# Five pairs of gate tiles from seven block products, ahead of the attention heads, in a transformer block in one kernel

## The chip, the cores and the metric

The kernel runs on one core of a Trainium2 chip. Its time is the device time of one execution in microseconds (us); the time before is the median of three runs. TensorE (PE) does the matrix products and its own weight loads (PEld), VectorE (DVE) and ScalarE (ACT) the elementwise work, GpSimd (POOL) a little of it, and SyncE (SP) issues nearly all DMA transfers, in order, on one queue.

## The reference

One transformer block over 1024 tokens of 1024 channels, 16 heads of 64, cut to what matters here:

```python
h = rms_norm(x, norm1_g)
glu_in, q, k, v, gate_logits = split(h @ w_in)        # 2048, 1024, 1024, 1024, 2048 columns
a = silu(rms_norm(causal_depthwise_conv(a_val * sigmoid(a_gate)), conv_norm_g))   # width 31
y_a = a @ w_conv_out
# q, k normed per head; three dilated windows (128/1, 512/4, 2048/16) with ALiBi,
# joined by their log-sum-exp: one softmax with a mask over all keys
o = attention(q, k, v)
y_b = o @ w_attn_out
g_a, g_b = split(sigmoid(gate_logits + gate_b))        # 1024 and 1024 columns
x = x + (g_a * y_a + g_b * y_b) @ w_out
x = x + feed_forward(rms_norm(x, norm2_g))             # 1024 -> 2 x 2816 -> 1024
```

All products are wanted in float32 accuracy. The kernel splits each factor into a rounded high part and the rest, and adds three products: high by high, high by low, low by high.

## The kernel before

**The gate product.** The logits of the gate are 16 tiles of 128 channels by 1024 tokens. For one tile and one half of the tokens `gemm_half` runs eight *steps*, one for each 128 input channels, of three matmuls with 512 columns (L111, L112, L113), 24 matmuls in all. The 16 tiles with their two halves are 768 matmuls. The conv output product `co` has eight such tiles, 384 matmuls. The generator `side_steps` lists both kinds in order, first the gates and then the conv output, 384 steps in all; each `next` issues one step. When a gate half is done, ACT copies it with the bias `C_GB` added (L210) and SP stores it to `dgate`; a tile's weights (`raw_gt`) are loaded ahead and split in four pieces, ACT rounding (`hi_gt`) and DVE subtracting (`lo_gt`), by `piece_high` and `piece_low`.

**Where the steps go.** After the q, k and v products, `cover` issues 43 of the steps (`COVER`) ahead of the heads, between the two small products of the conv branch's norm (`pss`, `psr`). 280 or so go into the heads: `FILL` gives for each of a head's eight slots how many steps are added, 17.5 a head, 60% of them before the slot's transposes and 40% after its output products. The rest, 37, run behind the last head, beside the first loads of the output projection.

**The heads.** A head has two halves of 512 queries, each half four slots of 128. In a slot, for queries i, `score` issues the products s (L697, L698), DVE adds the mask and takes the row minimum (L702), ACT does the exponential (L707), DVE the reciprocal (L710), and POOL scales the row (`share`, L711). Five slots later (`BACK`) the scaled rows are transposed on TensorE (`flip`, tile pp, L717), and ACT and DVE split the transposed block into `ph` (L79) and `pl` (L80). One slot on, `weigh` multiplies them by v (tile o, L731 and L732). The product has v's high and low part side by side as its 128 columns, so o holds two blocks of 64 rows which are added: `result` copies one with ACT to `ot` (L742), adds it on DVE (L743) and, for two heads together, stores the half to `do`. ACT's, DVE's and TensorE's instructions are issued in the order in which the code of this stage is written (`manual_schedule`); elsewhere a scheduler orders each engine.

**Around them.** A head's q, k and mask tiles are loaded by SP one head ahead, v half a head ahead. Before the heads, DVE does the width-31 convolution (L556) beside the q, k and v products. Behind the heads, `load_split` loads `do` half by half, splits it into `oT` and `merge` multiplies by the attention output weights; for that the gates are loaded and go through ACT's sigmoid.

The feed-forward's up-projection already works by pairs of tiles and seven block products; there `product` issues one block product of 12 matmuls (4 blocks of 128, three matmuls each).

Of the kernel before, what the change touches and what calls it, by code (L numbers as in the profile page):

```python
# [21 lines left out]
P = 128  # L22
D = 1024
# [12 lines left out]
FILL = (1.5, 3.4, 1.8, 1.9, 1.6, 3.0, 2.1, 2.2)  # L36
BACK = 5
SHARE = 0.6
COVER = (15, 8, 20)
# [14 lines left out]
def block_kernel(ctx: ExitStack, tc: tile.TileContext, x, xT, x0, g2, pack, mask,  # L54
# [76 lines left out]

    def spill(dst, src):
        sp.dma_start(dst.bitcast(F32), src.bitcast(F32))
# [7 lines left out]
    dv = [dr.tile([P, 8, 8, P], F32R, name=f"dv{i}") for i in range(2)]  # L141
    dgate = [dr.tile([P, T], F32, name=f"dgate{i}") for i in range(16)]
    da = dr.tile([P, KT, T], F32, name="da")
    dya = [dr.tile([P, T], F32, name=f"dya{i}") for i in range(8)]
    do_ = dr.tile([P, KT, T], F32, name="do")
# [33 lines left out]
    def side_steps(hT, da):  # L179
# [18 lines left out]
        def gate(c, half):  # L198
            def go(w):
                gp = bank_ps(f"gate_{c}_{half}")  # L200
                if c >= 12 and half == 1:
                    if not aT:
                        aT.extend(hb_tiles(hb1, "aT"))
                    ask_conv(0, 2 * (c - 12))
# [5 lines left out]
                act.activation(sg, gp, AF.Identity, bias=pk[:, C_GB + c : C_GB + c + 1])  # L210
# [19 lines left out]
        for c in range(12):  # L230
            for half in range(2):
                gate(c, half)
        for half in range(2):
            for c in range(12, 16):
                gate(c, half)
        for c0 in (0, 4):
            for half in range(2):
                for c in range(c0, c0 + 4):
                    conv_out(c, half)
# [5 lines left out]
        for i, (_, n, go) in enumerate(uses):  # L245
# [7 lines left out]
            if n.startswith("co"):  # L253
                need = max(need, marks[(i - 32) // 4 % 2])
# [25 lines left out]
    with tc.tile_pool(name="ph1", bufs=1) as p1:  # L280
# [157 lines left out]
        with tc.manual_schedule(engines={ENG.Activation, ENG.DVE, ENG.PE}):  # L438
# [30 lines left out]
            for k in range(KT):  # L469
# [5 lines left out]
                low(1, k)  # L475
                if k == 6:
                    factors(0)
# [13 lines left out]
            for k in range(KT):  # L491
# [3 lines left out]
                settled1 = low(0, k)  # L495
        pair(1, 1, range(8), HH + HL + LH, 1)
# [124 lines left out]
        p2i_cm = tc.tile_pool(name="ph2i", bufs=1, side="right", reuse_waits="tile")  # L621
        p2i = p2i_cm.__enter__()

        def head(h):
            hp, r, g8 = h // 2, (h % 2) * DH, h // 8
            q = p2i.tile([P, T], F32R, tag="q", bufs=2, name=f"q_{h}")
            kh = p2i.tile([P, T], F32R, tag="kh", bufs=2, name=f"kh_{h}")
            kl = p2i.tile([P, T], F32R, tag="kl", bufs=2, name=f"kl_{h}")
            m = p2i.tile([P, T], F32, tag="m", bufs=2, name=f"m_{h}")
# [7 lines left out]
        tiles = {0: head(0)}  # L637
        gates = side_steps(hT, da)

        def cover(n):  # L640
            for _ in range(n):
                next(gates)
                one_piece()

        cover(COVER[0])
# [12 lines left out]
        dgs = p1.tile([P, CW - 1 + T], F32, tag="apad", bufs=10, name="dgs")[:, 0:T].rearrange("p (a b) -> p a b", a=8)  # L658
        dve.tensor_tensor(out=dgs, in0=ident.unsqueeze(1).to_broadcast([P, 8, P]),
                          in1=rs8.unsqueeze(2).to_broadcast([P, 8, P]), op=ALU.mult)  # L660
        for tt in range(8):
            if tt % 4 == 0:
                psr = bank_ps(f"psr_{tt}")
            spread2 = pe.matmul(psr[:, (tt % 4) * P : (tt % 4 + 1) * P], ones, dgs[:, tt, :], start=True, stop=True)
            if tt % 4 == 3:
                dve.tensor_copy(sqacc[:, (tt // 4) * 512 : (tt // 4) * 512 + 512], psr)
        for c in range(8):
            ct = conv_acc[c]
            dve.tensor_tensor(out=ct, in0=ct, in1=sqacc, op=ALU.mult)
            ordered = conv_acc[c - 2] if c > 1 else p1.tile([P, CW - 1 + T], F32, tag="apad", bufs=10, name=f"ca_{c}")[:, 0:T]  # L670
            act.activation(turns(ordered), ct.rearrange("p (s m) -> p s m", s=2), AF.Silu,
                           scale=pk[:, C_CG + c : C_CG + c + 1])
            act.dma_start(da[:, c, :], ordered)
        cover(COVER[2])


    with tc.tile_pool(name="ph2", bufs=1, reuse_waits="tile") as p2:
# [3 lines left out]
        def ready2(tag, shape, dt, bufs, name):  # L681
            return laid.pop(tag) if tag in laid else p2.tile(shape, dt, tag=tag, bufs=bufs, name=name)

        def values(h):
            vals[h] = p2.tile([P, 8, P], F32R, tag="v", bufs=2, name=f"v_{h}")
# [38 lines left out]
        outs, opairs, read_out = {}, {}, {}  # L724
# [706 lines left out]
```

## Time and profile before

| | |
|---|---|
| time, three runs | 1744.08, 1743.93, 1745.34 us; median 1744.08 |
| span of the profiled execution (first to last instruction) | 1741.8 us, 2.3 us under the median of the runs |
| TensorE matmul busy | 1737.4 us (100%) |
| DVE, ACT, POOL busy | 1301.5 (75%), 797.1 (46%), 174.5 us (10%) |
| first gate step | 457.3 us |
| heads, first to last group of eight transposes for keys 0 of half 1 | 511.96 to 884.91 us |
| attention output product | from 928.5 us |

The profile is of one execution. A row of the timeline gives start, length, engine, line, operation, tile written and tiles read; matmuls are pipelined, so a row's length is longer than the distance to the next start, which is what counts. A row of a group has after its count the sum in us and the mean in ns.

### The profile page before, as it was taken

The numbers are of one execution on the slowest core, as the hardware profiler recorded it, in microseconds if no ns is written. First come the engines' busy times: TensorE is split into PE (matmuls) and PEld (weight loads), VectorE is DVE, ScalarE is ACT, GpSimd is POOL, SyncE is SP. The second block draws the span as 40 slices with busy tenths as digits, with TensorE's granted clock in tenths as the row PEclk, the third lists the DMA queues.
The fourth block names the chain that finished last, engine by engine and source line by source line (L and its number), as shares of the span: only waits on it lengthen the run. The fifth ranks groups of instructions, "written<-read, shape, count | busy, mean of one in ns | idle before, by whom it ended". The sixth has DMA issues, their size and how long they took to land.

```text
span 1741.8 us, 22805 instructions
## 1 busy us (share of the span) xinstructions
PE 1737.4 (100%) x8207; PEld 1449.2 (83%) x8207; DVE 1301.5 (75%) x2005; ACT 797.1 (46%) x1276; POOL 174.5 (10%) x188
## 2 busy tenths in 40 slices
PE   9999999999999999999999999999999999999999
PEld 7888888888888888888888888888888888888887
DVE  5999999999756666677654573787777776889873
ACT  5421233323276666667663342555445544633431
POOL 0000232132012222222200000000000000000000
PEclk9999999999999999999999999999999999999999
DMA  7211145345686456657456576632222222398851
GB/s 295 73 54 50 53 135 170 109 140 175 174 274 180 148 159 168 179 161 225 128 179 210 178 271 236 218 121 73 97 80 77 85 85 85 127 362 310 295 176 49
DMA packets 149633, 276.99 MB, mean 159 GB/s; under 512 B 12048, under 2 KB 61840, under 8 KB 149520
## 3 DMA queue, kind: packets, MB, share of 16 engines
q1 hardware_dynamic: 147072, 269.11, 47.1%
q10 hardware_dynamic: 2448, 6.42, 0.9%
q8 instruction: 64, 1.05, 0.2%
q14 instruction: 49, 0.40, 0.1%
HBM read 202.09 MB, written 73.40 MB: 158 GB/s over the span
## 4 chain that ended last, share of the span: by engine, by line
PE 99%; DMA 0%; SPq 0%; DVE 0%; issue 0%; ACT 0%; DVEq 0%; ACTq 0%
PE dx L1243 7%; PE xz L976 6%; PE xz L975 6%; PE xz L977 6%; PE dy L1243 5%; PE qkv L130 5%; PE qkv L128 5%; PE qkv L129 5%; PE pp L717 4%; PE gate L111 3%; PE gate L112 3%; PE gate L113 3%; PE y L976 2%; PE y L977 2%; PE y L975 2%; PE o L732 2%
## 5 line engine op out<-in xcount | busy, mean ns | idle before, releaser
L80 DVE TENSOR_TENSOR pl<-pp,ph 128x512 fp32r<-128x512 f32 (+2 forms) x191 | 100.2, 553 | 90.1 <-ACT ph L79 90.0
L128 PE MATMUL qkv<-hi_qkv,hT 128*128 128x512 f32 x384 | 151.0, 394 | 0.0
L130 PE MATMUL qkv<-hi_qkv,hT 128*128 128x512 f32 x384 | 150.2, 392 | 0.0
L129 PE MATMUL qkv<-lo_qkv,hT 128*128 128x512 f32 x384 | 149.6, 391 | 0.0
L79 ACT ACTIVATE ph<-pp 128x512 fp32r<-128x512 f32 (+2 forms) x191 | 86.7, 489 | 115.9 <-PE pp L717 115.6
L702 DVE CUSTOM_DVE_ANT_0 p<-s,m 128x128 f32<-128x128 f32 (+3 forms) x120 | 90.5, 754 | 44.1 <-PE s L698 39.7
L711 POOL TENSOR_SCALAR p<-p,st 128x128 f32<-128x128 f32 (+3 forms) x120 | 90.3, 752 | 281.7 <-DVE st L710 222.4
L1146 DVE SCALAR_TENSOR_TENSOR u<-u,pk 128x1023 f32<-128x1023 f32 x88 | 112.3, 1278 | 1.2 <-ACT u L1144 0.9
L111 PE MATMUL gate<-hT,hi_gt 128*128 128x512 f32 x256 | 102.3, 400 | 0.0
L112 PE MATMUL gate<-hT,hi_gt 128*128 128x512 f32 x256 | 100.4, 392 | 0.0
L113 PE MATMUL gate<-hT,lo_gt 128*128 128x512 f32 x256 | 100.3, 393 | 0.0
L104 POOL TENSOR_TENSOR rs<-ss,mhalf 128x8 f32<-128x8 f32 x32 | 67.0, 2096 | 295.7 <-DVE ss L103 295.6
L707 ACT ACTIVATE p<-p,st 128x128 f32<-128x128 f32 (+3 forms) x120 | 93.0, 775 | 2.7 <-DVE st L702 2.0
L556 DVE SCALAR_TENSOR_TENSOR cacc<-csum,both,cacc 128x512 f32<-128x512 f32 x120 | 89.5, 746 | 1.2 <-ACT cacc L554 0.9
L556 DVE SCALAR_TENSOR_TENSOR cacc<-apad,pk,cacc 128x512 f32<-128x512 f32 x120 | 87.6, 745 | 0.0
L130 PEld LDWEIGHTS qkv<-hi_qkv,hT 128*128 128x128 f32 x384 | 72.1, 188 | 14.9
L129 PEld LDWEIGHTS qkv<-lo_qkv,hT 128*128 128x128 f32 x384 | 72.2, 188 | 14.4
L80 DVE TENSOR_TENSOR lo_uv<-raw_uv,hi_uv 128x1024 fp32r<-128x1024 f32 x20 | 24.5, 1226 | 79.7 <-ACT hi_uv L79 79.7
L128 PEld LDWEIGHTS qkv<-hi_qkv,hT 128*128 128x128 f32 x384 | 72.1, 188 | 14.1
L556 DVE SCALAR_TENSOR_TENSOR codd<-apad,pk,codd 128x513 f32<-128x513 f32 x112 | 83.7, 748 | 0.0
L717 PE MATMUL pp<-ident,p 128*128 128x128 f32 x540 | 78.9, 273 | 0.0
L717 PEld LDWEIGHTS pp<-ident,p 128*128 128x128 f32 x540 | 65.6, 140 | 14.9 <-DVE pl L80 0.5
(370 smaller groups left out, 4846.3 us busy)
## 6 DMA issues: line engine op xcount, KB each, us to landing
wr<-w_down SPq DMA_DIRECT2D x45, 512.0 KB, 5.8
gr<-dff SPq DMA_DIRECT2D x62, 256.0 KB, 5.1
raw_qkv<-w_qkv SPq DMA_DIRECT2D x24, 512.0 KB, 4.4
dff<-u SPq DMA_DIRECT2D x22, 512.0 KB, 2.6
raw_uv<-w_up SPq DMA_DIRECT2D x21, 512.0 KB, 3.2
raw_ug<-w_up SPq DMA_DIRECT2D x20, 512.0 KB, 3.2
dv<-v SPq DMA_DIRECT2D x16, 512.0 KB, 3.2
raw_gt<-w_ch SPq DMA_DIRECT2D x16, 512.0 KB, 3.8
```

Source lines behind the costliest of these rows:

```text
L111: pe.matmul(o, hi[:, k, :], ah[:, k, :], start=(k == 0), stop=False)
L112: pe.matmul(o, hi[:, k, :], al[:, k, :], start=False, stop=False)
L113: pe.matmul(o, lo[:, k, :], ah[:, k, :], start=False, stop=(k == KT - 1))
L128: pe.matmul(ps, ah, hi[:, k % 2, :], start=(k == 0), stop=False)
L129: pe.matmul(ps, ah, lo[:, k % 2, :], start=False, stop=False)
L130: pe.matmul(ps, al, hi[:, k % 2, :], start=False, stop=(k == KT - 1))
L556: dve.scalar_tensor_tensor(out=out_, in0=src[:, i : i + size], scalar=w(i), in1=out_, op0=ALU.mult, op1=ALU.add)
L717: pe.transpose(pp[:, qb * P : (qb + 1) * P], pts[qb][:, kt * P : (kt + 1) * P], ident)
L975: pe.matmul(o, wh[:, k, :], bh[:, k, :], start=(start and k == 0), stop=False, skip_group_check=not start)
L976: pe.matmul(o, wh[:, k, :], bl[:, k, :], start=False, stop=False, skip_group_check=not start)
L977: end = pe.matmul(o, wl[:, k, :], bh[:, k, :], start=False, stop=(k == 3), skip_group_check=not start)
L1243: pe.matmul(banks[n][:, cols], a[:, c], b[:, d], start=(start and i == 0 and m == 0), stop=(stop and i == nf - 1 and m == 2), skip_group_c ...
```

## The change

Ten of the 16 gate tiles (`PAIRS`) are computed by pairs: the product of two tiles of channels by two halves of tokens, with the 1024 input channels in two halves, is a 2 by 2 block product, done with seven block products of 12 matmuls and a number of sums of blocks (Strassen's scheme in Winograd's form). Two tiles (`PLAIN`) are done as before, ahead of the pairs; the pairs' stage is ordered by hand on ACT, DVE and TensorE and ends before the heads; four tiles (`LATE`) and the conv output stay as filling of the heads, with a new `FILL` of 8.0 steps a head and one more in each of the first six slots (`FIRST`). For one factor of the products the normed tokens are stored to `dh` early, loaded again (eight loads of 512 KB), summed into four forms and split (`token_forms`); one quarter of the tokens' split, whose room the forms take, is spilled to `db12` and restored after the pairs. The weights of a pair are loaded, summed (`sums`) and split (`parts`). The steps of the conv branch's norm stand in the pairs 0 to 2. The tiles of head 0 are fetched when pair 3 begins.

`result` no longer adds the two blocks of 64 rows: ACT copies 128 rows, SP stores both blocks to two tensors `do` (for each half of two heads four stores of 64 rows where there was one of 128), and `load_heads` loads both and adds them on DVE (eight sums of 1024 columns) before the split. `ot` has four buffers instead of two. The gate's bias moves from the copy behind the product to the sigmoid in `merge`.

```diff
-FILL = (1.5, 3.4, 1.8, 1.9, 1.6, 3.0, 2.1, 2.2)
+FILL = (0.8, 2.2, 0.6, 0.6, 0.4, 1.7, 0.8, 0.9)
+FIRST = 1.0
 BACK = 5
 SHARE = 0.6
-COVER = (15, 8, 20)
+PLAIN = (10, 11)
+LATE = (12, 13, 14, 15)
+PAIRS = ((0, 1), (2, 3), (4, 5), (6, 7), (8, 9))
+COVER = 15
...
+    def product(o, wh, wl, bh, bl, start):
+
+        for k in range(4):
+            pe.matmul(o, wh[:, k, :], bh[:, k, :], start=(start and k == 0), stop=False, skip_group_check=not start)
+            pe.matmul(o, wh[:, k, :], bl[:, k, :], start=False, stop=False, skip_group_check=not start)
+            end = pe.matmul(o, wl[:, k, :], bh[:, k, :], start=False, stop=(k == 3), skip_group_check=not start)
+        return end
...
-                act.activation(sg, gp, AF.Identity, bias=pk[:, C_GB + c : C_GB + c + 1])
+                act.activation(sg, gp, AF.Copy)
...
+        for i in range(2):
+            spill(db12[i], hT[i][1][:, 0:4, :])
+        early_gates = side_steps(hT, da, PLAIN, ())
...
+        def gate_first(c, w):
+            xz = big_ps(f"gx_{c}")
+            for i in range(2):
+                product(xz[:, i * 512 : i * 512 + 512], four(w[0])[:, 4 * i : 4 * i + 4], four(w[1])[:, 4 * i : 4 * i + 4],
+                        *left[i], True)
+            return xz
...
+        def token_forms(i):
+            ks = slice(2 * i, 2 * i + 2)
+            view = lambda t: t.rearrange("p (a b) -> p a b", a=2)
+            load = lambda n, k, half: stage(dh[:, k + 2 * i : k + 2 * i + 2, half * 512 : half * 512 + 512], f"h{n}_{i}")
+            r22, r12, r11, r21 = (load(n, k, half) for n, k, half in (("22", 4, 1), ("12", 0, 1), ("11", 0, 0), ("21", 4, 0)))
+            tt = lambda o, a, b, op: dve.tensor_tensor(out=o, in0=a, in1=b, op=op)
+            tt(r22, r22, r12, sub)
+            tt(r12, r12, r11, sub)
+            tt(r11, r22, r11, add)
+            def rounded(dst, src):
+                split(dst[0][:, ks], dst[1][:, ks], view(src))
+
+            rounded(b12, r22)
+            rounded(form["t1"], r12)
+            tt(r21, r21, r11, sub)
+            rounded(form["t2"], r11)
+            return lambda: rounded(form["t4"], r21)
...
+        cover(COVER)
+        firsts = [gate_weights(a)[1] for a, _ in PAIRS[:2]]
+        N = len(PAIRS)
+        raws = [{} for _ in PAIRS]
+        pw = [{} for _ in PAIRS]
+        tiles = {}
+        tt_ = lambda o, a, b, op: dve.tensor_tensor(out=o, in0=a, in1=b, op=op)
+
+        def load(n, which):
+            raws[n][which] = stage(w_ch[16 + PAIRS[n][which]], f"g{which}_{n}")
+
+        def sums(n):
+            v, g = raws[n][0], raws[n][1]
+            s = raws[n][2] = wp.tile([P, 1024], F32, tag="raw", bufs=4, name=f"gs_{n}")
+            tt_(s[:, 0:512], g[:, 0:512], g[:, 512:], add)
+            tt_(s[:, 512:], s[:, 0:512], v[:, 0:512], sub)
+            tt_(g[:, 0:512], v[:, 0:512], g[:, 0:512], sub)
+            tt_(v[:, 512:], v[:, 512:], s[:, 512:], sub)
+
+        def parts(n, which, name):
+            src = raws[n][which] if which != "s4" else raws[n][0][:, 512:]
+            pw[n][name] = [four(t) for t in wsplit(src, f"{name}_{n}")]
+
+        ENG = mybir.EngineType
+        hand = {ENG.Activation, ENG.DVE, ENG.PE}
+        with tc.manual_schedule(engines=hand):
+            token_forms(0)()
+            fourth = token_forms(1)
+            load(0, 0)
+            load(0, 1)
+            sums(0)
+            parts(0, 2, "s12")
+            fourth()
+            parts(0, 1, "s3")
         with tc.issue_after(settled1.ins):
             conv_acc = conv_branch()
-
-
-        pss = bank_ps("pss")
-        for tt in range(8):
-            summed = pe.matmul(pss[:, tt : tt + 1], sqacc[:, tt * P : (tt + 1) * P], ones[:, 0:1], start=True, stop=True)
-        rs8 = p1.tile([P, 8], F32, name="crs8")
-        cs8 = p1.tile([P, 8], F32, name="css8")
-        rstd_of(rs8, pss[:, 0:8], D, cs8)
-        with tc.issue_after(summed.ins):
-            cover(COVER[1])
-        dgs = p1.tile([P, CW - 1 + T], F32, tag="apad", bufs=10, name="dgs")[:, 0:T].rearrange("p (a b) -> p a b", a=8)
-        dve.tensor_tensor(out=dgs, in0=ident.unsqueeze(1).to_broadcast([P, 8, P]),
-                          in1=rs8.unsqueeze(2).to_broadcast([P, 8, P]), op=ALU.mult)
-        for tt in range(8):
-            if tt % 4 == 0:
-                psr = bank_ps(f"psr_{tt}")
-            spread2 = pe.matmul(psr[:, (tt % 4) * P : (tt % 4 + 1) * P], ones, dgs[:, tt, :], start=True, stop=True)
-            if tt % 4 == 3:
-                dve.tensor_copy(sqacc[:, (tt // 4) * 512 : (tt // 4) * 512 + 512], psr)
-        for c in range(8):
-            ct = conv_acc[c]
-            dve.tensor_tensor(out=ct, in0=ct, in1=sqacc, op=ALU.mult)
-            ordered = conv_acc[c - 2] if c > 1 else p1.tile([P, CW - 1 + T], F32, tag="apad", bufs=10, name=f"ca_{c}")[:, 0:T]
-            act.activation(turns(ordered), ct.rearrange("p (s m) -> p s m", s=2), AF.Silu,
-                           scale=pk[:, C_CG + c : C_CG + c + 1])
-            act.dma_start(da[:, c, :], ordered)
-        cover(COVER[2])
-
-
-    with tc.tile_pool(name="ph2", bufs=1, reuse_waits="tile") as p2:
+        cover(16 * len(PLAIN) - COVER)
+        for _ in early_gates:
+            pass
+
+        xz, c11 = {}, {}
+
+        def begun(n):
+            c11[n] = quarter(f"c11_{n}")
+            act.activation(c11[n], xz[n][:, 0:512], AF.Copy)
+            tt_(c11[n], xz[n][:, 512:1024], c11[n], add)
+            sp.dma_start(dgate[PAIRS[n][0]][:, 0:512], c11[n])
+
+        with tc.manual_schedule(engines=hand):
+            for n in range(2):
+                xz[n] = gate_first(n, firsts[n])
+                begun(n)
+            load(1, 0)
+            for n, (a, b) in enumerate(PAIRS):
+                X = xz[n][:, 0:512]
+                Y = bank_ps(f"gy_{n}")
+                (sh, sl), (gh, gl) = pw[n]["s12"], pw[n]["s3"]
+                inner = 0 < n < N - 1
+                if n + 2 < N:
+                    load(n + 2, 0)
+                if n == 3:
+                    p1_cm.__exit__(None, None, None)
+                    p2_cm = tc.tile_pool(name="ph2", bufs=1, reuse_waits="tile")
+                    p2 = p2_cm.__enter__()
+                    pool2.append(p2)
+                    tiles[0] = head(0)
+                if n + 1 < N:
+                    load(n + 1, 1)
+                parts(n, "s4", "s4")
+                if inner:
+                    parts(n + 1, 0, "v")
+                product(X, sh[:, 4:8], sl[:, 4:8], *form["t2"], False)
+                c12 = quarter(f"c12_{n}")
+                act.activation(c12, X, AF.Copy)
+                product(Y, sh[:, 0:4], sl[:, 0:4], *form["t1"], True)
+                p5 = quarter(f"p5_{n}")
+                act.activation(p5, Y, AF.Copy)
+                if n == 0:
+                    rs8 = conv_factors()
+                if n == 1:
+                    conv_spread(rs8)
+                if 0 < n < 3:
+                    for c in range(4 * n - 4, 4 * n):
+                        conv_result(c)
+                product(X, gh[:, 0:4], gl[:, 0:4], *b12, False)
+                c22 = quarter(f"c22_{n}")
+                tt_(c22, X, p5, add)
+                sp.dma_start(dgate[b][:, 512:1024], c22)
+                if n + 1 < N:
+                    sums(n + 1)
+                if inner:
+                    xz[n + 1] = big_ps(f"gx_{n + 1}")
+                    for i in range(2):
+                        product(xz[n + 1][:, i * 512 : i * 512 + 512], *(t[:, 4 * i : 4 * i + 4] for t in pw[n + 1]["v"]),
+                                *left[i], True)
+                    parts(n + 1, 2, "s12")
+                    begun(n + 1)
+                else:
+                    product(Y, *pw[n]["s4"], *b22, False)
+                    tt_(c12, Y, c12, add)
+                    if n + 1 < N:
+                        parts(n + 1, 2, "s12")
+                product(X, gh[:, 4:8], gl[:, 4:8], *form["t4"], False)
+                c21 = quarter(f"c21_{n}")
+                act.activation(c21, X, AF.Copy)
+                sp.dma_start(dgate[b][:, 0:512], c21)
+                if inner:
+                    product(Y, *pw[n]["s4"], *b22, False)
+                if n + 1 < N:
+                    parts(n + 1, 1, "s3")
+                if inner:
+                    tt_(c12, Y, c12, add)
+                sp.dma_start(dgate[a][:, 512:1024], c12)
...
+        for i in range(2):
+            fetch(b12[i], db12[i])
...
-            if h % 2 == 0 and half == 0:
-                opairs[h // 2] = ready2("op", [P, T], F32, 2, f"op_{h}")
-            opair, o = opairs[h // 2], outs.pop((h, half))
+            o = outs.pop((h, half))
             cs = slice(half * 512, half * 512 + 512)
-            tmp = ready2("ot", [P, 512], F32, 2, f"ot_{h}_{half}")
-            read_out[h, half] = act.activation(tmp[r : r + DH, :], o[DH:P, :], AF.Copy)
-            dve.tensor_tensor(out=opair[r : r + DH, cs], in0=o[0:DH, :], in1=tmp[r : r + DH, :], op=ALU.add)
-            if h % 2 == 1:
-                sp.dma_start(do_[:, h // 2, cs], opair[:, cs])
+            tmp = ready2("ot", [P, 512], F32, 4, f"ot_{h}_{half}")
+            read_out[h, half] = act.activation(tmp, o, AF.Copy)
+            for i in range(2):
+                sp.dma_start(do_[i][r : r + DH, h // 2, cs], tmp[i * DH : (i + 1) * DH, :])
...
-                rate = FILL[at % 8] if cur else 4
+                rate = FILL[at % 8] + FIRST * (at < 6) if cur else 4
...
-        load_split(oT, do_, 0, "o")
+
+        def load_heads(half):
+            for k in range(0, KT, 2):
+                raw, low = (stage(do_[i][:, k : k + 2, half * 512 : half * 512 + 512], f"o{i}_{half}{k}") for i in range(2))
+                dve.tensor_tensor(out=raw, in0=raw, in1=low, op=ALU.add)
+                split(oT[0][half][:, k : k + 2, :], oT[1][half][:, k : k + 2, :], raw.rearrange("p (a b) -> p a b", a=2))
+
+        load_heads(0)
         ao_raw = [stage(w_ao[c], f"ao{c}") for c in range(2)]
-        load_split(oT, do_, 1, "o")
+        load_heads(1)
...
-                act.activation(ga, ga, AF.Sigmoid)
-                act.activation(gb, gb, AF.Sigmoid)
+                act.activation(ga, ga, AF.Sigmoid, bias=pk[:, C_GB + c : C_GB + c + 1])
+                act.activation(gb, gb, AF.Sigmoid, bias=pk[:, C_GB + 8 + c : C_GB + 9 + c])
```

More of the change, by code (lines that the diff above doesn't have):

```diff
@@ L141, in block_kernel @@
     dv = [dr.tile([P, 8, 8, P], F32R, name=f"dv{i}") for i in range(2)]
+    dh = dr.tile([P, KT, T], F32, name="dh")
+    db12 = [dr.tile([P, 4, 512], F32R, name=f"db12_{i}") for i in range(2)]
     dgate = [dr.tile([P, T], F32, name=f"dgate{i}") for i in range(16)]
@@ L620, in block_kernel, with cover @@
         p1a_cm.__exit__(None, None, None)
-        p2i_cm = tc.tile_pool(name="ph2i", bufs=1, side="right", reuse_waits="tile")
-        p2i = p2i_cm.__enter__()
+        pT_cm = tc.tile_pool(name="phT", bufs=1, side="right", reuse_waits="tile")
+        pT = pT_cm.__enter__()
+        for i in range(2):
+            spill(db12[i], hT[i][1][:, 0:4, :])
+        early_gates = side_steps(hT, da, PLAIN, ())
+        def cover(n):
+            for _ in range(n):
+                next(early_gates)
+                one_piece()
@@ L777, in block_kernel @@
                         values(h + 1)
-                    with ExitStack() as behind:
-                        if at == 0:
-                            behind.enter_context(tc.issue_after(spread2.ins))
-                        new = score(h, tiles[h], half * 4 + n)
+                    new = score(h, tiles[h], half * 4 + n)
                     pts[h, half, n] = new[0]
@@ L968, in block_kernel @@
                 transpose_raw(*tails.pop(0))
-        def product(o, wh, wl, bh, bl, start):
-            for k in range(4):
-                go = not start and k == 0
-                pe.matmul(o, wh[:, k, :], bh[:, k, :], start=(start and k == 0), stop=False, skip_group_check=not start)
-                pe.matmul(o, wh[:, k, :], bl[:, k, :], start=False, stop=False, skip_group_check=not start)
-                end = pe.matmul(o, wl[:, k, :], bh[:, k, :], start=False, stop=(k == 3), skip_group_check=not start)
-            return end
-        four = lambda t: t.rearrange("p (a b) -> p a b", b=P)
         left = [(lefts[i][:, 0], lefts[i][:, 1]) for i in range(2)]
```

112 lines of the change are left out of this document (82 added, 30 removed).

## Prediction

> **What bounds the kernel now.** I read the busy shares first, then the slices, then the chain that ended last.
>
> ```profile
> span 1741.8 us, 22805 instructions
> PE 1737.4 (100%) x8207; PEld 1449.2 (83%) x8207; DVE 1301.5 (75%) x2005; ACT 797.1 (46%) x1276; POOL 174.5 (10%) x188
> PEclk9999999999999999999999999999999999999999
> PE 99%; DMA 0%; SPq 0%; DVE 0%; issue 0%; ACT 0%; DVEq 0%; ACTq 0%
> ```
>
> TensorE is never without work, its granted clock is full in every slice, and 99% of the chain is TensorE. So the time is the sum of TensorE's issue times: a matmul that goes is a gain in full, and any wait put in front of TensorE is a loss in full, for there is no idle time to hide it. Every other engine has room on average; whether it has room at the right moment decides this case. The run times (median 1744.1) lie 2.3 us above the span; I keep that difference.
>
> Next come the issue intervals, from the timeline (first and last start of nine matmuls in a row), and the windows of the first products, the heads and what follows them (span in window, then busy time and count of PE, PEld, DVE, ACT, POOL).
>
> ```profile
> 457.30 0.39 PE L111 MATMUL gate<-hT,hi_gt 128*128 128x512 f32 x1
> ...
> 459.11 0.39 PE L111 MATMUL gate<-hT,hi_gt 128*128 128x512 f32 x1
> 40.00:60.00 20.00, 20.00 (x90) 16.55 (x89) 16.26 (x23) 12.54 (x18) 0.25 (x2) 1.00 0.31 104
> 550.00:600.00 50.00, 50.00 (x277) 42.77 (x276) 31.81 (x84) 30.23 (x68) 12.06 (x17) 1.00 0.59 173
> 860.00:910.00 50.00, 50.00 (x258) 42.17 (x258) 29.62 (x57) 32.91 (x63) 5.60 (x7) 1.00 0.44 145
> ```
>
> Eight intervals take 1.81 us: 0.2265 us a matmul of 512 columns (the 0.39 is its pipelined length). A step of three is 0.68 us. In the heads (550 to 600) DVE and ACT are busy 64% and 60%.
>
> The length of one head is read from the chain: its group of eight transposes for keys 0, half 1, comes once a head. Inside one head, from the timeline, one filling step and the head's two ends:
>
> ```profile
> 511.96 0.87 PE pp L717 x8
> ...
> 858.94 0.87 PE pp L717 x8
> 585.71 1.03 PE L717 MATMUL pp<-ident,p 128*128 128x128 f32 x8
> ...
> 599.10 0.39 PE L111 MATMUL gate<-hT,hi_gt 128*128 128x512 f32 x1
> ...
> 599.79 0.60 PE L717 MATMUL pp<-ident,p 128*128 128x128 f32 x4
> ...
> 610.83 1.04 PE L717 MATMUL pp<-ident,p 128*128 128x128 f32 x8
> ```
>
> Fourteen heads take 346.98 us: 24.78 a head, with 17.5 filling steps. The head from 585.71 to 610.83 had 18 and took 25.12. A step among transposes takes 0.69 here; over the 18 it is 0.70 on average, a little over 0.68, for the matmul behind a change of shape starts late.
>
> **The change, part by part.**
>
> *Matmuls.* A pair of gate tiles by seven block products is 7 x 12 = 84 matmuls instead of 96; five pairs save 60, so 60 x 0.2265 = **-13.6 us**.
>
> *Where they stand.* Ahead of the heads stood 43 steps, 129 matmuls; now 32 plain steps and 5 x 84, 516 matmuls: 387 x 0.2265 = +87.7. In the heads 9.5 steps a head go: the measured head of 25.12 less ten of its steps is 18.15, against 24.78: -6.63 x 16 = -106.1. The six extra steps at the first slots are +4.1; the rest after the heads is 34 steps, not 37: -2.0. The sum without a new wait is **-16.3**: the 13.6, and 2.7 because steps taken out of the heads run at the denser pace.
>
> *The thinner heads.* This is the term that I size least well. What a head asks of DVE and ACT hardly shrinks: 24.78 x 0.64 = 15.8 us of DVE, less two result adds at 0.68 and about half the weight splits (1.2 together with their ACT half), so some 14 of 18.15 us, 77%. The slowest place is behind s_7, the widest score:
>
> ```profile
> 704.22 0.39 PE L698 MATMUL s<-kl,q 128*128 128x512 f32 x1
> 704.45 0.39 PE L111 MATMUL gate<-hT,hi_gt 128*128 128x512 f32 x1
> 704.76 1.22 DVE L702 CUSTOM_DVE_ANT_0 p<-s,m 128x1024 f32<-128x1024 f32 x1 [1.04 <-PE s L698]
> 706.02 1.15 ACT L707 ACTIVATE p<-p,st 128x1024 f32<-128x1024 f32 x1
> 706.03 0.43 DVE L80 TENSOR_TENSOR pl<-pp,ph 128x256 fp32r<-128x256 f32 x1
> 706.37 1.42 DVE L164 TENSOR_TENSOR lo_gt<-raw_gt,hi_gt 128x512 fp32r<-128x512 f32 x1
> 707.08 0.19 ACT L707 ACTIVATION_READ_ACCUMULATOR p<-p,st 128x1 f32 x1
> 707.55 0.28 PE L732 MATMUL o<-pl,v 128*128 128x256 f32 x1
> 707.92 0.15 DVE L710 RECIPROCAL st<-st 128x1 f32<-128x1 f32 x1
> 708.24 1.12 POOL L711 TENSOR_SCALAR p<-p,st 128x1024 f32<-128x1024 f32 x1 [0.99 <-DVE st L710]
> 709.99 1.03 PE L717 MATMUL pp<-ident,p 128*128 128x128 f32 x8
> ```
>
> Call 704.45, where s_7 has been issued, E. DVE waits for the score, does the row minimum (704.76), then pl, which ends at 706.46 = E+2.01. TensorE wants that pl at 707.55 = E+3.10: slack 1.1. With the new FILL, one step lies between instead of three, and what stands there (transposes 0.14, o 0.43, a step 0.70, s_0 0.17, a transpose and the first o 0.2) lasts about 1.62: TensorE waits **0.39 us** a head. The longer chain from the same score (exp, reciprocal, POOL's share, transposes) ends at E+4.3 if the reciprocal follows exp at once; the transposes come at E+4.17 plus the 0.39, so it is covered by the first wait. A third place, the fifth group of transposes of half 1 waiting for its bank until pl has read it, I put by the same walk at 0 to 0.2. I take 0.5 a head, near the row that I could place, **+8.0** in all; the ends are 0 and the 1.6 of the rival below.
>
> *The forms and weights of the pairs.* All of it is hand ordered, so a late load holds DVE's whole queue (conv results and sums behind it) and TensorE. The rows: the gate weights' landing, from their tile's view, and groups by shape, the last two numbers before the idle time being the sum and the mean in ns.
>
> ```profile
> DMA to landing us min/median/max: 3.1/3.8/10.2
> ...
> L79 ACT ACTIVATE hi_uv<-raw_uv 128x1024 fp32r<-128x1024 f32 x20 | 21.2, 1059 | 34.3 <-PE xz L976 34.3
> ...
> L80 DVE TENSOR_TENSOR lo_uv<-raw_uv,hi_uv 128x1024 fp32r<-128x1024 f32 x20 | 24.5, 1226 | 79.7 <-ACT hi_uv L79 79.7
> L1007 DVE TENSOR_TENSOR raw_uv<-raw_uv,s 128x512 f32<-128x512 f32 x20 | 13.8, 692 | 0.6
> L1150 DVE TENSOR_TENSOR u<-u 128x1024 f32<-128x1024 f32 x22 | 26.8, 1220 | 1.6 <-ACT u L1149 1.6
> L743 DVE TENSOR_TENSOR op<-o,ot 64x512 f32<-64x512 f32 x28 | 19.1, 681 | 2.9 <-ACT ot L742 2.5
> ```
>
> The up-projection does these same operations. A pair asks of DVE four sums (2.8), three splits of 1024 columns (3.7), one of 512 (0.7) and three output adds (2.1): 9.2 of the pair's 84 x 0.2265 = 19.0 us on TensorE; with four conv products of 1.22 in two of the pairs, 14. That fits. The start is tight: the forms of the tokens are 8 x 1.22 + 8 x 1.23 = 19.6 us of DVE, and must be done, with pair 0's first weights, when TensorE has run the plain tiles (457.3 + 32 x 0.68 = 479.1) and the two first products of pairs 0 and 1 (10.9): 490.0. Pair 0's loads stand on SP behind the last plain gate's store. That store waits for the gate's last matmul and its copy, so the loads go at about 481 and 482.4, land 3.8 later, are summed (1.4), rounded by ACT (1.1) and subtracted (1.2), and with the semaphores between are ready at about 490.7: 0.7 late. The next product's are 0.3 early. I take **+0.7**, 0 to 4; a load as slow as the slowest gate weights' of before (first row: 3.1, 3.8, 10.2) would give the 4, for later pairs have some us of slack.
>
> *What costs nothing.* The gate's bias goes into a sigmoid that ran anyway. The store of the normed tokens (eight of 512 KB) goes out as they are made, around 40 to 60 us, where the DMA engines are 31% busy (the windows' last columns: clock, DMA share, GB/s). The result is one ACT copy of 128 rows instead of 64 (no more columns). Its adds (0.68 x 32 = 22 us) leave DVE in the heads and come back as eight of 1024 columns, 9.8 us, ahead of the output projection; there (860 to 910) DVE has 20 of 50 us free and 34 rest steps, 23 us, lie over the last loads, and half 0's eight tiles over half 1's. The SP issues added in the heads are four of 64 rows instead of one of 128 for two heads.
>
> ```profile
> raw_o<-do SPq DMA_DIRECT2D x8, 512.0 KB, 4.7
> ```
>
> For the first slots and the merge I add **+1** (0 to 5): there twice the bytes are fetched, and a piece late by one landing (raw_o took 4.7) would show in full.
>
> Sum: -16.3 + 8.0 + 0.7 + 1.0 = -6.6, so a span of 1735.2 and a time of **1737.5**.
>
> **The rivals.**
>
> *No new wait.* If pl and the share come a little sooner than I walked, as they may since DVE has fewer splits in its queue, the -16.3 stands: about 1728. For it speaks DVE's 23% of room; against it the 1.1 us of slack, of which 1.5 are taken.
>
> *The heads become bound by the softmax chain (slower).* In the rows above the reciprocal came at 707.92, E+3.47, not right behind the exp (707.27), for DVE was in a weight split of 1.42 us that ran beside POOL's share; the share ended at 709.36, E+4.91. If such a split still falls there, the transposes wait 0.74, not 0.39. When the pace is 2.27 us a slot instead of 3.1, the same may happen at a second score (s_3, with half 0's transposes) and at the banks: 0.74 + 0.6 + 0.2, about 1.6 a head, 25.6 in all; -16.3 + 25.6 + 1.7 = +11, **1755**. It decides from (16.3 - 1.7 + 3.5) / 16 = 1.1 us a head on. Against it: only half as many splits remain.
>
> *The pairs' weights come late.* SP issues in order, and each pair's loads stand behind stores that wait for products. Two pairs late by 4 us each bring 8: the time is then about 1745, no difference. Here a rule bears: the Trainium skill ("TensorE: Matmul & The Clock Gate", Part 1) has the clock halved after an idle window of some 3.4 us, and full again only after as long of work. By it, the two waits would cost an estimated 1.7 more each, 1748. No row here can show it: the clock line has no other digit than 9.
>
> **How the numbers follow.** 0.2% (3.5 us) is about what a measurement of this kernel can tell from no change. Forecast 0.55, spread over 1732 to 1742; no new wait 0.18; late weights 0.12; chain-bound heads 0.15. Faster takes no new wait, nearly all of the forecast and a little of the late weights: 0.73. Same takes the rest of the forecast and most of the late weights: 0.13. Slower is the chain-bound case without its mildest part and the worst late weights: 0.14. The range leaves out the far part of the chain-bound case, 0.1, and a little below: 1727 to 1749.
>
> **What would show it.** 60 fewer matmuls; the pitch of the eight transposes at 18.4 to 18.8 us (18.15: no wait; over 19.3: chain-bound); TensorE waiting for pl behind s_7, about 0.4; the first s12 product starting at 490 to 491. A PE idle over 3 us in the pairs, or a clock under 9, would make the forecast wrong at the weights; a pitch as forecast with another time would make it wrong at the ends.

## The result

The changed kernel takes 1747.67 us (median of 20 runs, 1745.61 to 1754.91) against 1744.68 us (20 runs, 1743.54 to 1745.82): a ratio of 1.0022, 95% interval 1.0016 to 1.0029. It is slower by 3 us, where 6.6 us less were forecast. Its runs also spread over 9 us, those of before over 2.

The page of the profile after (its span is 8.3 us longer than before; this execution is the second slowest of the 20):

```profile
span 1750.1 us, 22916 instructions
PE 1733.1 (99%) x8147; PEld 1440.5 (82%) x8147; DVE 1333.5 (76%) x2032; ACT 812.6 (46%) x1284; POOL 174.6 (10%) x188
PE 93%; DMA 3%; DVE 2%; issue 1%; ACT 0%; SPq 0%; POOL 0%; ACTq 0%; DVEq 0%
```

There are the 60 matmuls fewer. But 7% of the chain is no longer TensorE: DMA, DVE and issue came in. That is not all idle time, for the chain also runs through loads beside which TensorE still works. The waits of TensorE (engine, line, who ended them, total, times, longest; weight loads are counted separately) say where:

```profile
PE gy L139 <- ACT p L822: 4.6, 1, 4.6
PE o L922 <- DVE pl L84: 2.1, 5, 0.4
PE pp L907 <- POOL p L901: 1.2, 1, 1.2
...
PE gx L139 <- ACT hi_s L83: 0.9, 1, 0.9
PE gx L141 <- DVE lo_s L84: 0.5, 1, 0.5
```

The largest is one wait in the last pair, and nothing in the prediction had priced it. Followed back in the chain, and then in the timeline:

```profile
552.00 7.96 DMA kh<-dk
559.98 12.22 DMA q<-dq
572.27 7.85 DMA dgate<-c
580.22 0.60 ACT p L822
580.87 0.80 PE gy L139
581.66 0.43 PE gy L140
```

```profile
580.22 0.60 ACT L822 ACTIVATE p<-gy 128x512 f32<-128x512 f32 x1 [8.99 <-DMA dgate<-c]
580.87 0.80 PE L139 MATMUL gy<-hT,hi_s 128*128 128x512 f32 x1 [4.63 <-ACT p L822]
```

ACT's copy of pair 4's fifth product writes to a buffer whose former tenant, pair 3's c12, was still being stored. That store was issued at 572.27, after the loads of heads 0 and 1 (DVE had finished its tile at 568.15, 4.1 us before), and took 7.85 us to land. The copy waited, and with it the bank that the next product needs. The windows show both the jam and what the wait did to the clock:

```profile
570.00:575.00 5.00, 5.00 (x25) 4.17 (x24) 1.50 (x4) 1.22 (x3) 0.00 (x0) 1.00 1.02 320
575.00:580.00 5.00, 1.23 (x6) 0.69 (x4) 0.00 (x0) 0.00 (x0) 0.00 (x0) 0.94 1.05 424
580.00:585.00 5.00, 4.13 (x10) 3.27 (x11) 0.69 (x1) 2.37 (x4) 0.00 (x0) 0.50 0.95 397
585.00:590.00 5.00, 5.00 (x22) 4.08 (x21) 1.10 (x4) 1.12 (x3) 0.38 (x1) 0.88 0.41 141
```

The DMA engines are busy without a gap (share 1.0). Behind the 4.6 us of idle the granted clock is 0.50, and a matmul takes 0.43 us instead of 0.23 (581.66 to 582.09 in the chain): twelve of them, 580.87 to 586.15, cost 2.6 us more.

The heads, by the group of eight transposes that comes behind the one read before the change (that one has its wait inside and is not whole in the chain; the distance from head to head is the same):

```profile
609.56 0.87 PE pp L907 x8
628.36 0.88 PE pp L907 x8
...
875.51 0.87 PE pp L907 x8
```

The first interval is 18.80; fourteen heads take 265.95 us, 19.00 each. Without a wait it should be 18.15.

### The profile page after: what moved, and what is told of

Read it like the earlier page. It is cut to its first block, busy times and chain, and to the rows that moved or that the text cites. A ratio compares the mean times of both kernels' runs of the same rounds, so it can differ in the third digit from the quotient of the medians.

```text
span 1750.1 us, 22916 instructions
## 1 busy us (share of the span) xinstructions
PE 1733.1 (99%) x8147; PEld 1440.5 (82%) x8147; DVE 1333.5 (76%) x2032; ACT 812.6 (46%) x1284; POOL 174.6 (10%) x188
## 4 chain that ended last, share of the span: by engine, by line
PE 93%; DMA 3%; DVE 2%; issue 1%; ACT 0%; SPq 0%; POOL 0%; ACTq 0%; DVEq 0%
PE dx L1425 7%; PE xz L139 6%; PE xz L141 6%; PE xz L140 6%; PE dy L1425 5%; PE qkv L134 5%; PE qkv L132 5%; PE qkv L133 5%; PE pp L907 4%; PE y L141 2%; PE y L139 2%; PE y L140 2%; PE o L922 2%; PE s L888 2%; PE s L887 2%; PE o L921 2%
## 5 line engine op out<-in xcount | busy, mean ns | idle before, releaser
L921 PE MATMUL o<-ph,v 128*128 128x512 f32 (+2 forms) x191 | 74.1, 392 | 0.0
L922 PE MATMUL o<-pl,v 128*128 128x512 f32 (+2 forms) x191 | 66.0, 354 | 3.7 <-DVE pl L84 2.1
L139 PE MATMUL xz<-blk_t,hi_s3g 128*128 128x512 f32 x176 | 68.7, 390 | 0.0
```

The source lines that it names most:

```text
L139: pe.matmul(o, wh[:, k, :], bh[:, k, :], start=(start and k == 0), stop=False, skip_group_check=not start)
L921: pe.matmul(o[:, c], v[:, kt, :], ph[:, c], start=(kt == 0), stop=False)
```

## The experiments

All experiments start from the changed kernel. Each was timed beside the kernel before on the same chip; ratios are against it.

**The buffer of P5.**

```diff
+            if name == "p5_4":
+                return pool2[0].tile([P, 640], F32, tag="p4", bufs=1, name=name)[:, 0:512]
             if pool2:
```

> Pair 4's P5 copy writes to a buffer that nothing else holds (the room of a score row, free until the heads), so it no longer waits for the store of pair 3's c12. Theory A (a store in a jam of transfers holds the buffer, ACT, then TensorE; the idle time also lowers the clock): the idle of 4.8 us at 576 and the half clock behind it (2.5 us) are gone, no other wait of over 1 us takes their place before the heads; span about 1742.5, median about 1744.5, the runs within 1.5 us of each other. Rival B (the stall is an accident of the profiled run, the typical run loses its time in the heads): median stays at 1747 to 1748.

Measured: 1744.01 us, ratio 1.0001 (0.9992 to 1.0009), span 1741.6. The wait and the half clock are gone, with the DMA engines as full as before (one window of this run):

```profile
575.00:580.00 5.00, 5.00 (x24) 4.18 (x23) 1.80 (x5) 1.12 (x3) 0.37 (x1) 1.00 1.04 426
```

So it was the held buffer, not the traffic as such. It costs 3.7 us in the median, or 2.9 when each of the two is compared with the kernel before that was timed beside it (the profiled execution caught 8.5). The runs lie between 1742.6 and 1748.2, less spread than with the wait, but not the 1.5 us that I expected.

**Head 1's loads later.**

```diff
-                        tiles[h + 1] = head(h + 1)
+                        with tc.issue_after(third.ins) if h == 0 else ExitStack():
+                            tiles[h + 1] = head(h + 1)
```

(`third` is the store of pair 3's c12.)

> The seven loads of head 1 (2 MB) are put behind the store of pair 3's c12 in SP's queue; the buffers are as in the changed kernel. Theory A: that store goes about 5 us sooner and lands in 4 to 5 us instead of 7.9, the stall shrinks from 4.8 to under 1 us and the clock stays full: median 1744 to 1745. If instead the amount of transfers between 550 and 590 us counts and not their order, a stall of the same size comes back at the first slots (v, or the restored tokens): median 1747 to 1749.

Measured: 1746.54 us, ratio 1.0016 (1.0008 to 1.0025). The second expectation holds in kind: the stall at 576 is gone, as theory A says, and a wait came at 588, at a first score that waits for the row minimum two slots before it. The waits between 580 and 600 us, that minimum in the timeline with what it waited for in the chain, and the windows:

```profile
PE s L889 <- DVE st L894: 2.6, 1, 2.6
```

```profile
576.08 13.47 DMA dgate<-c
...
589.72 0.69 DVE L894 CUSTOM_DVE_ANT_0 p_first<-s,m 128x512 f32<-128x512 f32 x1 [4.34 <-DMA dgate<-c]
```

```profile
588.00:590.00 2.00, 0.00 (x0) 0.00 (x0) 0.28 (x1) 0.00 (x0) 0.00 (x0) 1.00 1.05 421
...
592.00:594.00 2.00, 2.00 (x7) 1.51 (x6) 1.70 (x2) 1.60 (x4) 0.68 (x1) 0.50 0.78 205
```

What the minimum waited for is neither v nor the restored tokens: it writes to a score row whose room is one of the pairs' output buffers, and that buffer's store took 13.47 us to land. So it is the same mechanism at another buffer. Reordering the queue chose who waits; a wait of 2.6 us also halved the clock.

**Head 0's tiles one pair later** (`n == 3` becomes `n == 4`; with that the buffers of the last pair are new ones too, so this run is not of one cause).

> As the changed kernel, but head 0's tiles are fetched when pair 4 begins, one pair (19 us) later. Theory A (the early fetch is needed, and its price is the jam): the stores of pair 3 land in 4 us, no wait for the buffer of P5, but the first scores wait for their tiles, 3 to 10 us: median 1748 to 1753. If the early fetch was not needed: no wait at the first scores, median 1743 to 1745.

Measured: 1749.35 us, ratio 1.0031 (1.0019 to 1.0043). The median lies where theory A has it, but the first scores did not wait 3 to 10 us, so it is wrong in its place. P5's buffer is not waited for any more. The profiled execution (span 1744.5, the fastest of its runs) shows waits of 1.4 us for a gate weight and 0.9 for v. What the slower runs lose is not seen in any trace, so this run does not show what the early fetch is worth.

**One step moved behind s_7.**

```diff
-FILL = (0.8, 2.2, 0.6, 0.6, 0.4, 1.7, 0.8, 0.9)
+FILL = (0.8, 1.2, 0.6, 0.6, 0.4, 1.7, 0.8, 1.9)
```

> One filling step a head is moved from behind s_1 to behind s_7 (FILL's second value 2.2 to 1.2, its last 0.9 to 1.9), the sum stays 8.0. If the wait for pl is a loss of its own (theory of the prediction): TensorE no longer waits 0.4 us for pl, the pitch of a head falls from 18.83 to about 18.45, median 6 us lower. If the chain exp, reciprocal, POOL's share, transposes behind s_7 binds (rival): the pl wait goes, but the eight transposes wait 0.6 to 0.7 instead of 0.24, pitch still 18.8, median unchanged.

Measured: 1749.92 us, ratio 1.0031 (1.0019 to 1.0043). The rival holds in its mechanism: TensorE does not wait for pl any more, but for POOL's scaled row instead. The interval is 18.77 to 19.25: 18.8, as the rival has it, in four of the first thirteen heads, and 19.2 in nine. In exactly those nine a subtraction of a weight or conv piece, 1.24 us long, stands ahead of s_7's row minimum on DVE (more of this below). The chain, and the timeline at the group just ahead of the second of these:

```profile
602.09 0.87 PE pp L907 x8
620.86 0.88 PE pp L907 x8
639.64 0.88 PE pp L907 x8
658.88 0.87 PE pp L907 x8
```

```profile
617.91 0.49 PE L907 MATMUL pp<-ident,p 128*128 128x128 f32 x3
618.84 0.77 PE L907 MATMUL pp<-ident,p 128*128 128x128 f32 x5 [0.44 <-POOL p L901]
```

Three transposes run, the fourth, of s_7's row, comes 0.6 us late. A step put inside the span of a chain but taken from the same span gained nothing here (the step behind s_1 stood ahead of these transposes too).

**One step more behind s_7** (last value 1.9, sum 9.0).

> One more filling step a head behind s_7 (FILL's last value 1.9, sum 9.0), 16 steps fewer behind the last head. If both waits behind s_7 are short of one step of 0.70 us: both are hidden, the pitch is 18.85 with nine steps, so the 16 steps (10.9 us) come out of the end: 9 to 11 us less than the changed kernel, median 1737 to 1739, if the 18 steps left at the end still cover the loads of the output projection. If DVE or ACT is what a head is bound by: pitch 19.5, no gain.

Measured: 1754.67 us, ratio 1.0066 (1.0053 to 1.0080). Neither median came. In the first heads the pitch is as expected with nine steps (18.88), so the waits are hidden there; in five heads of the middle it is 19.2, 19.2, 20.2, 20.3 and 19.7. But 16 steps were taken from the end, and there TensorE waited for the output projection's weights, whose rounding stands on ACT behind the late head outputs. The waits of its TensorE, and one window behind the 2.1 (its columns as before, the clock third from the end):

```profile
PE yb L115 <- ACT hi_ao L83: 6.0, 1, 6.0
PE pp L907 <- DVE pl L84: 3.4, 2, 2.1
```

```profile
866.00:870.00 4.00, 3.78 (x14) 3.37 (x15) 1.92 (x6) 2.75 (x6) 1.41 (x2) 0.57 0.66 171
```

The clock is 0.50 for 7 us behind the 6.0, and for 3.4 us behind the 2.1, which is in head 14, where DVE stood 2.95 us for the load of the first of the later adds. The 34 steps at the end are a cover that is used.

**One step from behind s_5 to behind s_7, with e1's buffer.**

```diff
-FILL = (0.8, 2.2, 0.6, 0.6, 0.4, 1.7, 0.8, 0.9)
+FILL = (0.8, 2.2, 0.6, 0.6, 0.4, 0.7, 0.8, 1.9)
```

> P5 of pair 4 in its own buffer as in e1_own_buffer, and one filling step a head moved from behind s_5 (FILL 1.7 to 0.7) to behind s_7 (0.9 to 1.9); the sum stays 8.0, so the end keeps its 34 steps. If a head is bound only by the chain behind s_7 (4.8 us from s_7's last matmul to the eight transposes, of which 4.15 are filled): both waits go, pitch 18.2 instead of 18.83, 15 x 0.65 = 10 us less than e1_own_buffer, median 1734. If the steps behind s_5 cover a chain of their own (s_3's, half 0's transposes) or DVE and ACT bind: pitch 18.6 to 18.9, median 1741 to 1744.

Measured: 1737.84 us, ratio 0.9969 (0.9957 to 0.9980). The pitch is 18.2 in nine of the heads, as predicted for a chain behind s_7 alone, and 18.95 in heads 5 to 8. From the chain (its first head; the fifth):

```profile
601.76 0.87 PE pp L909 x8
...
619.96 0.87 PE pp L909 x8
...
693.50 0.87 PE pp L909 x8
712.44 0.88 PE pp L909 x8
```

So 6.2 of the 10 us came. What stands ahead of s_7's row minimum on DVE in one of those four, from the timeline:

```profile
704.99 0.91 POOL L903 TENSOR_SCALAR p<-p,st 128x768 f32<-128x768 f32 x1 [1.87 <-DVE st L902]
705.22 1.21 DVE L180 TENSOR_TENSOR aT<-raw_a,aT 128x512 fp32r<-128x512 f32 x1
...
706.36 1.21 DVE L894 CUSTOM_DVE_ANT_0 p<-s,m 128x1024 f32<-128x1024 f32 x1
```

In exactly these four heads a subtraction of the conv output's factors stands there. It takes 1.21 us while POOL scales a row (until 705.90), against 0.68 alone.

**The adds back in the heads, with e1's buffer.**

```diff
+            read_out[h, half] = act.activation(tmp[r : r + DH, :], o[DH:P, :], AF.Copy)
+            dve.tensor_tensor(out=both[r : r + DH, :], in0=o[0:DH, :], in1=tmp[r : r + DH, :], op=ALU.add)
+            sp.dma_start(do_[0][r : r + DH, h // 2, cs], both[r : r + DH, :])
...
-        load_heads(0)
+        load_split(oT, do_[0], 0, "o")
```

> As e1_own_buffer, but the two blocks of a head's output are added on DVE in the heads, as before the change (one ACT copy of 64 rows, one add, one store of 64 rows a half), and the output projection's tokens come by eight loads without adds. If the heads are bound by the chain behind s_7 and not by DVE's load: pitch unchanged at 18.8, and the 1.6 us wait in head 14 (DVE held by the first of the later adds, which waits for its load) is gone: median 1 to 2 us under e1_own_buffer, 1742 to 1743. If DVE's load counts: pitch 19.1 to 19.5, 5 to 10 us more, 1749 to 1754.

Measured: 1750.08 us, ratio 1.0033 (1.0021 to 1.0046): 6 us more than e1_own_buffer, as the second expectation has it. Two heads take 38.42 instead of 37.66 us. DVE is busy 173.5 of 220 us (165.0 in e1_own_buffer). The chain, one window over the heads, and two waits of TensorE's weight loads between 600 and 860 us:

```profile
602.04 1.00 PE pp L909 x8
640.46 1.03 PE pp L909 x8
```

```profile
620.00:840.00 220.00, 215.60 (x1224) 180.12 (x1224) 173.52 (x455) 167.19 (x379) 68.09 (x90) 1.00 0.72 194
```

```profile
PEld o L923 <- DVE op L934: 3.1, 13, 0.3
PEld pp L909 <- DVE pl L84: 1.8, 11, 0.2
```

Neither of these two waits is in e1_own_buffer. About once a head the next product o waits for an add that reads o, and a group of transposes for a pl that stands on DVE; at 0.24 and 0.16 us they make about the 0.38 a head. So the adds cost by where they stand on DVE; whether its total load costs as well is not shown. This part of the change is worth those 6 us.

**The later adds out of head 14's chain.** On e5_fill_moved:

```diff
+                with tc.issue_after(shared[8 * 15 - 1].ins):
+                    dve.tensor_tensor(out=raw, in0=raw, in1=low, op=ALU.add)
```

(`shared` lists the reciprocals in the order of the slots.)

> As e5_fill_moved, and the adds of the head outputs are queued on DVE behind the last reciprocal of head 14, so that DVE does not stand waiting for their load in the middle of head 14's chain. Theory: the wait of 1.3 to 1.6 us in head 14 goes and nothing else changes: 1 to 1.5 us under e5_fill_moved. If the room that the loaded pieces hold is needed by the conv output's weights, a wait of some us appears at ya instead.

Measured: 1736.56 us, ratio 0.9960 (0.9948 to 0.9973), 1.3 less than e5_fill_moved; with both medians uncertain by about 2 us this agrees, but the difference alone isn't shown. Head 14's interval goes from 20.02 to 19.32 us, 0.7 less: the wait of 1.6 us for POOL's row is gone, but one of 0.9 for pl came, for the add, 1.91 us long where it overlaps POOL, stands ahead of that pl.

**No split ahead of s_7's minimum.** On e8_fill_moved_add_later:

```diff
-                piece_low()
+                if at % 8 < 6:
+                    piece_low()
```

> As e8_fill_moved_add_later, and no low part of a weight or conv piece is subtracted on DVE in the slots of s_6 and s_7 (it goes to the next slot, s_0). In heads 5 to 8 of e5_fill_moved such a subtraction stood ahead of s_7's row minimum and lasted 1.21 us beside POOL's scaling, against 0.68 alone. Theory: with it out of the chain the pitch of these heads falls from 18.95 to 18.2, 4 x 0.75 = 3 us: median 1733.5. If ACT's copies of the same pieces, or the loads, make these heads longer: pitch stays 18.9, median as e8_fill_moved_add_later, 1736.5.

Measured: 1735.75 us, ratio 0.9950 (0.9938 to 0.9963). The pitch of heads 5 to 8 is 18.66, where 18.2 was expected and 18.95 stood: about 0.3 of 0.75, with a wait for POOL's row in its place. The timeline, in the head before these four and in the first of them:

```profile
670.09 1.12 POOL L903 TENSOR_SCALAR p<-p,st 128x1024 f32<-128x1024 f32 x1 [0.38 <-DVE st L902]
...
688.24 1.62 POOL L903 TENSOR_SCALAR p<-p,st 128x1024 f32<-128x1024 f32 x1 [0.39 <-DVE st L902]
688.28 0.68 DVE L180 TENSOR_TENSOR aT<-raw_a,aT 128x512 fp32r<-128x512 f32 x1
```

The subtraction left the row minimum alone, but in its new slot it starts 0.04 us after POOL begins to scale s_7's row, and that scaling takes 0.50 us more, in each of these four heads and in none of the four before them. This is read from the trace, not tested by a run; it is the size of the 0.46 that the pitch keeps above 18.2.

**The conv norm's small products ahead of pair 0.** On e9_no_split_at_s7, `conv_factors` moves from behind P5 to ahead of pair 0's first product.

> As e9_no_split_at_s7, and the sixteen small matmuls of the conv norm (pss, 1.7 us of TensorE) stand ahead of pair 0's first s12 product, whose weights came 0.5 to 1.8 us late in all runs so far. Theory: they fill that wait, 1.0 to 1.5 us less than e9_no_split_at_s7, the product still starts at about 492. If the factors' DVE step, now ahead in DVE's queue, holds up the weights behind it: no gain, the wait moves to the third product.

Measured: 1733.82 us, ratio 0.9942 (0.9928 to 0.9955): the fastest version, 10.6 us under the kernel before. No wait at s12 is left in its trace; the difference from e9_no_split_at_s7 (1.9 us) is of the expected size and within what the runs can tell.

## Why the prediction was wrong

The forecast was 1737.5, the result 1747.7: 10.2 us off, and the sign with it. Three terms make it up.

*The forms and weights of the pairs, +0.7 (0 to 4).* The step that failed: I walked the loads of the weights and the forms, and priced neither head 0's and 1's loads on SP nor the pairs' five output buffers, each of which is free only when its store has landed. "Late weights" was a rival, but as loads behind stores, with 0.12; it was a store behind loads. It cost 3.7 us in the median. The same wait is 4.6 us in the profile after, 2.0 in e3_cover_pl's and 1.5 in e4_more_fill's, which have the same code up to there. With the half clock behind the longer ones, that fits the spread of the changed kernel's runs: the six slowest (1749.45 us and more) all have a mean granted clock under 1.000, and three of the other fourteen do. The sign that I had named, a PE idle of over 3 us in the pairs, did come, but at an output buffer and not at the weights.

The clock of 0.50 behind these waits is where a rule of the Trainium skill came true ("TensorE: Matmul & The Clock Gate", Part 1: the clock is halved after an idle window of some 3.4 us, until there is a busy one). The traces agree on the half clock, but it came already behind 2.6 us of idle (e2_head1_later) and 2.1 (e4_more_fill), while 2.0 left it at 1.00 (e3_cover_pl). My estimate of 1.7 us a wait was low for the profile after: it took 2.6.

*The thinner heads, +8.0.* The base was exact: with the waits gone the pitch is 18.19 (e5_fill_moved) against my 18.15. The wait for pl behind s_7 was 0.40 where I had 0.39. The timeline of the profile after:

```profile
640.56 0.39 PE L888 MATMUL s<-kl,q 128*128 128x512 f32 x1
642.32 0.40 DVE L84 TENSOR_TENSOR pl<-pp,ph 128x256 fp32r<-128x256 f32 x1
642.78 0.39 PE L922 MATMUL o<-pl,v 128*128 128x256 f32 x1
643.64 0.16 DVE L900 RECIPROCAL st<-st 128x1 f32<-128x1 f32 x1 [0.71 <-ACT p L897]
643.97 1.47 POOL L901 TENSOR_SCALAR p<-p,st 128x1024 f32<-128x1024 f32 x2 [0.38 <-DVE st L900]
644.64 1.27 PE L907 MATMUL pp<-ident,p 128*128 128x128 f32 x8
```

What failed, and it is the largest of the three, is the next step: "the transposes come at E+4.17 plus the 0.39, so it is covered by the first wait". E is 640.79 here, and the group starts at 644.64 = E+3.85 with the 0.40 in it; the fourth transpose, the first that needs s_7's row, would come 0.33 later, at E+4.18. So with the wait for pl in it the place is the 4.17 that I had without it: adding the 0.39 on top counted it twice. The chain's end at E+4.3 was right, so the transposes wait as well: 0.24, the group taking 1.03 instead of 0.79. So it is 0.65 a head and not 0.5. Two more things added to that: 0.3 a head in heads 5 to 8, where splits delay the minimum (in exactly these four a subtraction of 1.24 us stands ahead of it, as in the rows of e5_fill_moved), and 1.1 in head 14, where DVE stood 0.62 us for a load of the later adds. That is (19.00 - 18.65) x 14 = 4.9 us more than I had in fourteen heads. The rival of the chain-bound heads had its mechanism right (e3_cover_pl: the chain sets the pitch, not pl) and its size wrong: 0.85 a head on average, under the 1.1 from which it would have decided alone.

*The first s12 product* came at 491.29, not 490.7, and its low part 0.7 late: 1.8 in place of 0.7.

Together 3.7 + 4.9 + 1.1 = 9.7 of the 10.2. The sum is rougher than it looks: 0.6 of the 10.2 is the kernel before, which took 1744.68 beside the changed one and not 1744.08; the buffer's price is 2.9 against the kernels before timed beside each; and in e1_own_buffer's profile the s12 product lost 1.1, not 1.8.

*What costs nothing* was wrong in both directions. The adds that left the heads, to which the forecast gave no price of their own, are a gain of 6 us (e6_sum_in_heads); and the later adds took head 14's 1.1. The 0.68 of a subtraction that became 1.21 beside POOL agrees with the Trainium skill ("SBUF — State Buffer", "SBUF: two separate sides": a DVE instruction with two SBUF inputs and a GpSimd one that reads SBUF lock each other out): it ends 0.53 us after POOL does. The agreement is in kind: after a full block it would have ended 0.68 behind POOL, and in e9_no_split_at_s7 the same meeting made POOL's scaling longer (1.62 instead of 1.12) and left the subtraction at 0.68.

Right were the 60 matmuls, the 18.15, the place and size of the pl wait, the gain that is there without waits (e10_pss_first has still waits and is 10.6 us faster, of the 16.3 in the sum; the rest is not shown), and the ends (0.5 us of wait at the first slots and 0.4 at the merge in the profile after, +1 forecast).

Open: what makes e7_head0_later's typical runs 3 us slower than its profiled one.

## What to carry to other kernels

When work is taken out from between the links of a chain, place what is left by the chain: count from its start to each consumer, once, and put the filling where the longest link has none; the sum of the filling matters less than its slot. Price every transfer that a change brings forward against every buffer that is freed by a store on the same queue. And where TensorE has no idle time, one wait of a few us costs its length and, behind each of the four waits of 2.1 us or more in these traces, the half clock.

## What the runs showed of the hardware

The granted clock fell to 0.50 behind idle times of 2.1 (e4_more_fill), 2.6, 4.6 and 6.0 us, and not behind 2.0 or the shorter ones; four such waits are too few to call the step between 2.0 and 2.1 a threshold. Behind the 2.6 it fell only 1.0 us after the matmuls had begun again. Matmuls ran at it for 3.4 to 6.7 us. A 256 KB store among loads that kept the DMA engines at a share of 1.0 took 7.85 us to land, and one in e2_head1_later 13.47; the median of the 32 gate stores in the kernel before was 3.9. Where a DVE subtraction of 0.68 us met POOL's scaling of a row, one of the two took 0.5 us longer: the subtraction in e5_fill_moved, the scaling in e9_no_split_at_s7.
